# A memory-bound batch norm: phases of three tiles, stores held behind a gate, parameters loaded as rows

## The chip, the cores and the metric

The kernel runs on one core of one Trainium2 chip. The metric is the device time of one execution in microseconds; lower is better. A trace shows one execution of a kernel, so a table made from traces can differ by a few us from the medians: the traced execution of the kernel before took 2490.18 us, the slowest of its runs.

## The reference, cut to what matters

```python
# x: (32, 256, 128, 128) float32; gamma, beta, running_mean, running_var: (256,)
def reference(x, gamma, beta, running_mean, running_var):
    eps = 1e-5
    # all four reshaped to (1, -1, 1, 1)
    return gamma * (x - mean) / np.sqrt(var + eps) + beta
```

It is one multiply and one add for each element. 536.9 MB are read and as many written. A tile is 128 channels of one image: 128 rows of 16384 floats, 64 KiB a row, 8.39 MB. There are 64 tiles, and three fit on chip.

## The kernel before, the parts that matter

```python
NBUF = 3
def issue_load(i):
    t = data.tile([P, HW], mybir.dt.float32, tag="t")
    loads[i] = nc.sync.dma_start(out=t[:], in_=xr[i])
    tiles[i] = t

for i in range(NBUF):
    issue_load(i)

def load_param(ap_1d):                      # four times, 4 bytes an element
    t = params.tile([P, NCB], mybir.dt.float32, tag=ap_1d.tensor.name)
    nc.gpsimd.dma_start(out=t, in_=ap_1d.rearrange("(j p) -> p j", p=P))
    return t
# ... scale and shift from the parameters; compute(i): one tensor_scalar in place

K = NBUF - 1
for b in range((NT + K - 1) // K):
    idxs = [i for i in range(K * b, K * b + K) if i < NT]
    for i in idxs:
        compute(i)
    for i in idxs:
        store(i)                            # also on the sync queue
    for i in idxs:
        issue_load(i + NBUF)                # waits for the store of tile i
```

Loads and stores share one queue, so each of the 16 DMA engines works through them in this order: loads 0, 1, 2, stores 0, 1, loads 3, 4, stores 2, 3, and so on. I call a place where this order goes from loads to stores or back a *turn*.

## Time and profile before

| | before |
|---|---|
| time, median of 3 runs | 2487.14 us (2486.58 to 2490.18) |
| span of the profiled run | 2488.1 us |
| VectorE busy | 564.7 us, 23% |
| DMA | 9 tenths or more in all slices but the last, 432 GB/s |

From the page of the kernel before: busy times (engine, us, share, instructions), the rate in 40 equal slices, the group of the compute, and the issues with their median time from issue to landing.

```profile
DVE 564.7 (23%) x69; ACT 1.6 (0%) x2; POOL 3.2 (0%) x8
...
GB/s 414 429 438 433 433 429 437 436 430 431 435 436 433 428 437 436 434 428 436 433 437 428 435 435 435 426 437 436 435 427 435 436 438 426 434 437 436 432 431 378
...
L86 DVE TENSOR_SCALAR t<-t,scale_t,shift_t 128x16384 f32<-128x16384 f32 x64 | 564.0, 8812 | 1868.0 <-DMA t<-in_x_dram 1867.9
...
t<-in_x_dram SPq DMA_DIRECT2D x64, 38.6
out_dram<-t SPq DMA_DIRECT2D x64, 49.9
```

Nothing computes for long, VectorE waits for loads, and the rate is flat except at both ends.

The end, in windows of 4 us (window: length, three engines' busy us, clock, DMA share, GB/s):

```profile
2474.00:2478.00 4.00, 0.00 (x0) 0.00 (x0) 0.00 (x0) 1.00 0.80 344
2478.00:2482.00 4.00, 0.00 (x0) 0.00 (x0) 0.00 (x0) 1.00 0.45 197
2482.00:2486.00 4.00, 0.00 (x0) 0.00 (x0) 0.00 (x0) 1.00 0.23 98
```

The rate runs out over some 10 us, since the engines do not end together. (A packet is counted whole in the window where it begins, so single windows of a few us swing above and below 434 GB/s.)

**Splitting the packet records by engine.** The trace records each DMA packet with start, duration and bytes, but no engine number. On one engine a packet nearly always starts 3 to 4 ns before its predecessor's recorded end, and the sequence of sizes is known from the kernel's order. Chaining the records by these two rules gave 16 chains of exactly the expected length with no record left over. "Loss" is always a packet's time above the median packet of its size. In the kernel before the median 64 KiB packet takes 2.418 us, so 1024 packets an engine take 2476.0 us: that is the floor, and 12 us, 0.5%, lie above it.

### The profile page before, as it was taken

How to read it: one execution, taken by the hardware profiler on the slowest of the kernel's cores; microseconds unless marked ns; L12 is line 12 of the kernel's file. 1: busy time of each engine (PE TensorE's matmuls, PEld its weight loads, DVE VectorE, ACT ScalarE, POOL GpSimd, SP SyncE). 2: the span in 40 equal slices, each digit the busy share in tenths (PEclk: the TensorE clock that was granted, in tenths of full speed). 3: DMA queues.
4: the chain of work that ended last, by engine and by line, in shares of the span. 5: the costliest groups of instructions: out<-in, count | busy, mean ns of one | idle time of the engine just before them, and what ended most of it. 6: DMA issues, size and time to landing. Idle time of an engine off the chain costs nothing.

```text
span 2488.1 us, 378 instructions
## 1 busy us (share of the span) xinstructions
DVE 564.7 (23%) x69; ACT 1.6 (0%) x2; POOL 3.2 (0%) x8
## 2 busy tenths in 40 slices
DVE  2122211222112221122212222121221212212121
ACT  0000000000000000000000000000000000000000
POOL 0000000000000000000000000000000000000000
DMA  9999999999999999999999999999999999999998
GB/s 414 429 438 433 433 429 437 436 430 431 435 436 433 428 437 436 434 428 436 433 437 428 435 435 435 426 437 436 435 427 435 436 438 426 434 437 436 432 431 378
DMA packets 18562, 1073.77 MB, mean 432 GB/s; under 512 B 2176, under 2 KB 2176, under 8 KB 2176
## 3 DMA queue, kind: packets, MB, share of 16 engines
q1 hardware_dynamic: 18432, 1073.75, 99.8%
q0 software_dynamic: 128, 0.00, 0.0%
q14 instruction: 2, 0.02, 0.0%
HBM read 536.88 MB, written 536.87 MB: 432 GB/s over the span
## 4 chain that ended last, share of the span: by engine, by line
DMA 51%; another core or an unknown queue 36%; DVE 11%; SPq 0%; issue 0%; POOL 0%; DVEq 0%; POOLq 0%; PEldq 0%
DMA t<-in_x_dram 48%; DVE t L86 11%; DMA out_dram<-t 2%; DMA t<-in_running_mean_dram 1%; SPq L97 0%; POOL t L56 0%; DVEq L86 0%; POOLq L133 0%; SPq L48 0%; DVE shift_t L81 0%; DVE tmp_t L80 0%; DVEq L80 0%; PEldq L133 0%
## 5 line engine op out<-in xcount | busy, mean ns | idle before, releaser
L86 DVE TENSOR_SCALAR t<-t,scale_t,shift_t 128x16384 f32<-128x16384 f32 x64 | 564.0, 8812 | 1868.0 <-DMA t<-in_x_dram 1867.9
L78 DVE RECIPROCAL tmp_t<-tmp_t 128x2 f32<-128x2 f32 x1 | 0.2, 166 | 13.2 <-ACT tmp_t L71 13.2
L80 DVE TENSOR_TENSOR tmp_t<-t,scale_t 128x2 f32<-128x2 f32 x1 | 0.2, 160 | 7.6 <-DMA t<-in_running_mean_dram 7.6
L71 ACT ACT_TABLE_LOAD x1 | 1.3, 1283 | 12.4 <-DMA t<-in_running_var_dram 12.4
L79 DVE TENSOR_TENSOR scale_t<-t,tmp_t 128x2 f32<-128x2 f32 x1 | 0.2, 160 | 3.2 <-DMA t<-in_gamma_dram 3.2
L56 POOL DMA_DIRECT2D t<-in_running_var_dram x1 | 0.8, 839 | 0.8 <-PEq L133 0.8
L56 POOL DMA_DIRECT2D t<-in_gamma_dram x1 | 0.7, 722 | 0.0
L56 POOL DMA_DIRECT2D t<-in_beta_dram x1 | 0.7, 722 | 0.0
L56 POOL DMA_DIRECT2D t<-in_running_mean_dram x1 | 0.7, 722 | 0.0
L71 ACT ACTIVATE tmp_t<-t,eps_t 128x2 f32<-128x2 f32 x1 | 0.3, 295 | 0.0
L65 DVE MEMSET eps_t<- 128x1 f32 x1 | 0.1, 59 | 0.8 <-PEq L122 0.8
L81 DVE TENSOR_TENSOR shift_t<-t,tmp_t 128x2 f32<-128x2 f32 x1 | 0.2, 160 | 0.0
L122 POOL MEMSET const-bfloat16-1.0<- 128x1 bf16 x1 | 0.1, 96 | 0.0
L122 POOL MEMSET const-uint8-127<- 128x1 uint8 x1 | 0.1, 94 | 0.0
L122 POOL MEMSET const-float32-0.0<- 128x1 f32 x1 | 0.1, 93 | 0.2 <-issue 0.2
L122 POOL MEMSET const-float32-1.0<- 128x1 f32 x1 | 0.1, 93 | 0.0
## 6 DMA issues: line engine op xcount, KB each, us to landing
t<-in_x_dram SPq DMA_DIRECT2D x64, 38.6
out_dram<-t SPq DMA_DIRECT2D x64, 49.9
t<-in_running_var_dram POOLq DMA_DIRECT2D x1, 1.0 KB, 11.1
t<-in_gamma_dram POOLq DMA_DIRECT2D x1, 1.0 KB, 15.2
t<-in_beta_dram POOLq DMA_DIRECT2D x1, 1.0 KB, 19.5
t<-in_running_mean_dram POOLq DMA_DIRECT2D x1, 1.0 KB, 21.6
```

What stands on the lines that cost most here:

```text
L56: nc.gpsimd.dma_start(out=t, in_=ap_1d.rearrange("(j p) -> p j", p=P))
L65: nc.vector.memset(eps_t, eps)
L71: nc.scalar.activation(out=tmp_t[:], in_=var_t[:], func=mybir.ActivationFunctionType.Sqrt, bias=eps_t[:], scale=1.0,)
L78: nc.vector.reciprocal(out=tmp_t[:], in_=tmp_t[:])
L79: nc.vector.tensor_mul(out=scale_t[:], in0=gamma_t[:], in1=tmp_t[:])
L80: nc.vector.tensor_mul(out=tmp_t[:], in0=mean_t[:], in1=scale_t[:])
L81: nc.vector.tensor_sub(out=shift_t[:], in0=beta_t[:], in1=tmp_t[:])
L86: nc.vector.tensor_scalar(out=t[:], in0=t[:], scalar1=scale_t[:, cb : cb + 1], scalar2=shift_t[:, cb : cb + 1], op0=mybir.AluOpType.mult, ...
L122: nc = _bacc.Bacc("TRN2", target_bir_lowering=False, num_devices=1)
```

## The change

Its intent: fewer turns, three loads and then three stores; no store before all engines have nearly finished the phase's loads, so that reads and writes do not mix; and parameters read as four rows of 1 KiB instead of single floats. The core of the diff:

```diff
+GROUPS = [3] * 20 + [2, 2]
+LAST = 3072
...
+    def load_group(first, size):
+        for i in range(first, first + size - 1):
+            load(i, [HW])
+        return load(first + size - 1, [HW - LAST, HW])[0]     # two DMAs, 52 and 12 KiB a row
...
-        nc.gpsimd.dma_start(out=t, in_=ap_1d.rearrange("(j p) -> p j", p=P))
+    for r, ap in enumerate((running_var, gamma, beta, running_mean)):
+        nc.scalar.dma_start(out=rows[r : r + 1, :], in_=ap.rearrange("(o c) -> o c", o=1))
+    # ... nc.vector.transpose and four tensor_copy bring them to 128 partitions
...
+    for g, size in enumerate(GROUPS):
+        idxs = range(first, first + size)
+        for i in idxs:
+            compute(i)                                        # as many pieces as the load
+        for i in idxs:
+            s = store(i)
+            if i == first:
+                tc.add_manual_dep(s.ins, gate.ins.name, after, reason="stores after loads")
+        first += size
+        if g + 1 < len(GROUPS):
+            gate = load_group(first, GROUPS[g + 1])
```

The gate is the landing, on all 16 engines, of the 52 KiB piece of the phase's last load. When it opens, an engine that is exactly on time has eight packets of 12 KiB left, 3.7 us.

More of the change, by code (lines that the diff above doesn't have):

```diff
@@ L7 @@
 from concourse._compat import with_exitstack
-SINGLE_QUEUE = True
 NBUF = 3
+GROUPS = [3] * 20 + [2, 2]
+LAST = 3072
 @with_exitstack
@@ L26 @@
     eps = 1e-5
+    f32 = mybir.dt.float32
     N, C, H, W = x.shape
@@ L33 @@
     NT = N * NCB
+    B = 32
+    NQ = P // B
+    assert sum(GROUPS) == NT and max(GROUPS) <= NBUF
     params = ctx.enter_context(tc.tile_pool(name="params", bufs=1))
@@ L39 @@
     outr = out.rearrange("n (cb p) h w -> (n cb) p (h w)", p=P)
+    ctx.enter_context(tc.manual_schedule())
     tiles = {}
-    loads = {}
-    def issue_load(i):
-        if i >= NT:
-            return
-        t = data.tile([P, HW], mybir.dt.float32, tag="t")
-        loads[i] = nc.sync.dma_start(out=t[:], in_=xr[i])
-        tiles[i] = t
-    for i in range(NBUF):
-        issue_load(i)
-    def load_param(ap_1d):
-        t = params.tile([P, NCB], mybir.dt.float32, tag=ap_1d.tensor.name)
-        nc.gpsimd.dma_start(out=t, in_=ap_1d.rearrange("(j p) -> p j", p=P))
-        return t
@@ L59, with load @@
-    var_t = load_param(running_var)
-    gamma_t = load_param(gamma)
-    beta_t = load_param(beta)
-    mean_t = load_param(running_mean)
-    eps_t = params.tile([P, 1], mybir.dt.float32, tag="eps")
-    nc.vector.memset(eps_t, eps)
-    scale_t = params.tile([P, NCB], mybir.dt.float32, tag="scale")
-    shift_t = params.tile([P, NCB], mybir.dt.float32, tag="shift")
-    tmp_t = params.tile([P, NCB], mybir.dt.float32, tag="tmp")
+    def load(i, cuts):
+        t = data.tile([P, HW], f32, tag="t")
+        tiles[i] = t, cuts
+        return [
+            nc.sync.dma_start(out=t[:, a:b], in_=xr[i][:, a:b])
+            for a, b in zip([0, *cuts], cuts)
+        ]
@@ new lines, in load_group @@
+    def load_group(first, size):
+        for i in range(first, first + size - 1):
+            load(i, [HW])
+        return load(first + size - 1, [HW - LAST, HW])[0]
+    rows = params.tile([B, C], f32, tag="rows")
+    nc.vector.memset(rows, 0.0)
+    for r, ap in enumerate((running_var, gamma, beta, running_mean)):
+        nc.scalar.dma_start(out=rows[r : r + 1, :], in_=ap.rearrange("(o c) -> o c", o=1))
+    gate = load_group(0, GROUPS[0])
+    eps_t = params.tile([P, 1], f32, tag="eps")
@@ new lines @@
+    nc.vector.memset(eps_t, eps)
+    turned = params.tile([B, C], f32, tag="turned")
+    nc.vector.transpose(out=turned[:], in_=rows[:])
+    par = params.tile([P, NCB, 4], f32, tag="par")
+    blocks = turned.rearrange("p (cb q r) -> p cb q r", cb=NCB, q=NQ)
+    for q in range(NQ):
+        nc.vector.tensor_copy(out=par[q * B : (q + 1) * B], in_=blocks[:, :, q, 0:4])
+    var_t, gamma_t, beta_t, mean_t = (par[:, :, r] for r in range(4))
+    scale_t = params.tile([P, NCB], f32, tag="scale")
@@ L71 @@
+    shift_t = params.tile([P, NCB], f32, tag="shift")
+    tmp_t = params.tile([P, NCB], f32, tag="tmp")
     nc.scalar.activation(
         out=tmp_t[:],
-        in_=var_t[:],
+        in_=var_t,
         func=mybir.ActivationFunctionType.Sqrt,
@@ L78 @@
     nc.vector.reciprocal(out=tmp_t[:], in_=tmp_t[:])
-    nc.vector.tensor_mul(out=scale_t[:], in0=gamma_t[:], in1=tmp_t[:])
-    nc.vector.tensor_mul(out=tmp_t[:], in0=mean_t[:], in1=scale_t[:])
-    nc.vector.tensor_sub(out=shift_t[:], in0=beta_t[:], in1=tmp_t[:])
+    nc.vector.tensor_mul(out=scale_t[:], in0=gamma_t, in1=tmp_t[:])
+    nc.vector.tensor_mul(out=tmp_t[:], in0=mean_t, in1=scale_t[:])
+    nc.vector.tensor_sub(out=shift_t[:], in0=beta_t, in1=tmp_t[:])
     def compute(i):
-        t = tiles[i]
+        t, cuts = tiles[i]
         cb = i % NCB
-        nc.vector.tensor_scalar(
-            out=t[:],
-            in0=t[:],
-            scalar1=scale_t[:, cb : cb + 1],
-            scalar2=shift_t[:, cb : cb + 1],
-            op0=mybir.AluOpType.mult,
-            op1=mybir.AluOpType.add,
-        )
-    def store(i):
-        t = tiles.pop(i)
-        (nc.sync if SINGLE_QUEUE else nc.scalar).dma_start(out=outr[i], in_=t[:])
-    K = NBUF - 1
-    for b in range((NT + K - 1) // K):
-        idxs = [i for i in range(K * b, K * b + K) if i < NT]
+        for a, b in zip([0, *cuts], cuts):
+            nc.vector.tensor_scalar(
+                out=t[:, a:b],
+                in0=t[:, a:b],
+                scalar1=scale_t[:, cb : cb + 1],
+                scalar2=shift_t[:, cb : cb + 1],
+                op0=mybir.AluOpType.mult,
+                op1=mybir.AluOpType.add,
+            )
+    def store(i):
+        t, _ = tiles.pop(i)
+        return nc.sync.dma_start(out=outr[i], in_=t[:])
+    after = mybir.DependencyInfo(mybir.DependencyClass.Sync, mybir.DependencyReason.DATA)
+    first = 0
+    for g, size in enumerate(GROUPS):
+        idxs = range(first, first + size)
         for i in idxs:
@@ L104 @@
         for i in idxs:
-            store(i)
-        for i in idxs:
-            issue_load(i + NBUF)
+            s = store(i)
[4 more added lines that the diff above has]
+            gate = load_group(first, GROUPS[g + 1])
 _INS = ['x', 'gamma', 'beta', 'running_mean', 'running_var']
```

## The prediction

> **What bounds the kernel now.** The 16 DMA engines. The page's busy table gives VectorE 23% (64 x 8.81 us), the other compute engines 0%; its slices give DMA 9 tenths throughout, 432 GB/s. I split the trace's DMA packet records by engine (each packet follows the one that ended just before it). Each engine moves 1024 packets of 64 KiB. The median takes 2.418 us, loads and stores alike, so 1024 take 2476.0 us: 27.1 GB/s an engine, 434 in all. The Trainium skill (DMA: Bandwidth & Descriptors, "Where 436 GB/s comes from") puts the fabric's ceiling at 435.2 GB/s; this trace agrees within 0.4%. The span is 2488.1 us, so only some 12 us (0.5%) can be won:
> - 1.8 us before the first packet, 1.2 us after the last: they stay.
> - Packets above 2.418 us: 9.9 us on the slowest engine, 1 to 2 us on the fastest. The fastest end at 2477.7, the slowest at 2486.9 us; the windows view shows 213 GB/s and less after 2476 us.
>
> About 0.5 to 1 us an engine is lost on its first packet and another 0 to 1 us in the first 20 us, beside the parameters' 4-byte packets (the page counts 2176 under 512 B). Nearly all the rest sits in the last packet of the second load of a pair, just before stores: fast engines already store while slow ones still read, and the slow ones' packet takes 0.2 to 1.0 us more (about 0.27 us a turn over 31 turns). Turns from stores to loads cost next to nothing.
>
> **What the change does.**
> 1. Turns from loads to stores: 32 become 22. The order, one transfer after another, was already two loads, two stores.
> 2. The gate opens when the slowest engine has finished the first part of the last tile; 8 x 12 KiB an engine are left, 3.6 us at 27.1 GB/s. Landing comes 0.6 us after an engine's last packet, and issue to first packet took 1.0 us at the start, so stores reach the engines after about 1.6 us: no bubble on the slowest engine, idling only on engines that lead by over 2 us. The spread, which grew from 1.4 to 9.8 us, is held near 2 us. Mixing remains, since engines with a smaller lead still store while others read.
> 3. Splitting adds 176 packets an engine; at 9 ns or less each (what 2.418 us exceeds 65536 B at the skill's rate by; an estimate) 1.6 us.
> 4. Parameters: ready at 25 us now, perhaps 8 us after. Off the path, since loads fill the queue until 63 us; the small packets' disturbance goes, 0.5 us.
>
> **Sum.** Of the slowest engine's 8.4 us at turns, fewer turns save 2.5 us; the gate perhaps 1 to 3 more; parameters 0.5; splitting costs 1.6. I predict 2484 us (range 2479.5 to 2490). Faster by over 2%: 0.01; within 2%: 0.97; slower by over 2%: 0.02.
>
> **What would show it.** Median 64 KiB packet still 2.42 us; DMA at 9 tenths in every slice; engines' ends within 3 us, the last windows full; excess on the slowest engine 5 to 7 us, still before stores.
>
> **What would make it wrong.** If the gate's stores arrive later than 3.6 us, all engines idle 22 times. If the small spread makes reads collide with stores at every turn (0.8 us x 22), the time is 2495. If it prevents the collision, 2480.

## More of the kernel before

All runs quoted here were at a granted clock of 1.0.

A store lands 49.9 us after its issue although one transfer takes 19.3 us: it stood in the queue behind others, and the DMA engines always had work waiting.

The waits of SyncE, the engine whose queue issues all loads (L48) and stores (L97): line that waited, what for, us in total, times, longest.

```profile
SPq L48 <- DMA out_dram<-t: 1484.0, 61, 30.2
SPq L97 <- DVE t L86: 919.2, 33, 46.4
```

## The result

| | before | after |
|---|---|---|
| median of 5 runs | 2487.04 us (2486.45 to 2490.18) | 2494.43 us (2493.09 to 2495.65) |
| span of the profiled run | 2488.1 | 2493.9 |

The ratio is 1.0026, 95% interval 1.0014 to 1.0038: slower by about a quarter of a percent, well within 2%, but outside the predicted range. (A ratio is the mean time of one kernel's fast runs over that of the other's in the same rounds, so it is not quite the ratio of the medians.)

The page of the kernel after, the lines that answer to those above:

```profile
DVE 570.2 (23%) x97; ACT 1.6 (0%) x2; POOL 0.2 (0%) x4
...
GB/s 421 437 433 426 436 436 434 427 435 432 438 425 435 424 436 435 431 428 437 427 431 436 422 437 430 427 429 431 426 440 428 434 431 430 434 428 433 429 429 405
...
L103 DVE TENSOR_SCALAR t<-t,scale_t,shift_t 128x16384 f32<-128x16384 f32 (+2 forms) x86 | 568.2, 6628 | 1866.7 <-DMA t<-in_x_dram 1813.1
...
t<-in_x_dram SPq DMA_DIRECT2D x22, 6656.0 KB, 54.9
t<-in_x_dram SPq DMA_DIRECT2D x22, 1536.0 KB, 58.4
out_dram<-t SPq DMA_DIRECT2D x64, 41.9
```

The slices still look full. The last one rose from 378 to 405 GB/s, so the end is better; the middle is a little lower. Stores now land 41.9 instead of 49.9 us after issue, because they are issued later. The waits of SyncE:

```profile
SPq L114 <- DMA t<-in_x_dram: 1186.6, 22, 55.1
SPq L54 <- DMA out_dram<-t: 1026.0, 60, 19.0
SPq L114 <- DVE t L103: 182.1, 22, 8.7
```

The first line is the gate: 22 times the stores (L114) waited for a load to land. In one phase the timeline shows it (start us, us from the first issue to the end of the last, engine, line, out<-in):

```profile
1908.83 8.81 DVE L103 TENSOR_SCALAR t<-t,scale_t,shift_t 128x16384 f32<-128x16384 f32 x1 [10.56 <-DMA t<-in_x_dram]
1924.76 9.41 SPq L114 DMA_DIRECT2D out_dram<-t  x3
```

The phase's first two tiles are computed by 1917.6, but their stores are issued at 1924.8. The end:

```profile
2482.00:2486.00 4.00, 0.00 (x0) 0.00 (x0) 0.00 (x0) 1.00 0.98 426
2486.00:2490.00 4.00, 0.00 (x0) 0.00 (x0) 0.00 (x0) 1.00 0.83 360
2490.00:2494.00 4.00, 0.00 (x0) 0.00 (x0) 0.00 (x0) 1.00 0.04 16
```

The gate did what it was meant to do for the engines' unity: they now end within 2.2 us (2490.4 to 2492.6) instead of 9.2 (2477.7 to 2486.9). But the mean engine ends 9.7 us later. Where those went, in us an engine (mean of the 16), from the packet records:

```
                                              before    after
packets at the median time of their size      2476.0   2477.4
loss in the last load before stores             3.78     4.32   (both pieces of a split load)
loss in the last store before loads             0.01     6.91
loss in the first load after stores             0.09     2.10
loss elsewhere, the start included              1.22     1.21
idle (gaps over 60 ns)                          1.27     0.59
end: mean engine                              2481.3   2491.0
end: slowest engine                           2486.9   2492.6
```

Splitting costs 1.4 us. The turns from stores to loads, which had been free, cost 9.0. Evening out the engines' ends gives back 4.0 (the slowest engine was 5.6 us behind the mean and is now 1.6). What little idleness shows is no larger than before. So the question is why the last 64 KiB store packet before a load, 58 us after the gate, became slower.

Three theories:

- **Spread**: engines held close together meet each turn at the same moment and hinder each other.
- **Address**: at these turns the tile just written and the tile read next are now neighbours (k and k+1); in the kernel before they were always two apart.
- **Read-ahead**: an engine reads ahead of what it writes. When the stores are issued late, its read side has nothing to do for a moment and its lead is gone. The next reads from memory are then not hidden. The Trainium skill (DMA: Bandwidth & Descriptors, "Two DMAs through the same engine are not ordered") says that descriptors of one queue start in order but are pipelined, and that the read and the write side of an engine are separate queues; this makes such a lead possible. It states no length for it.

Read-ahead was formed after the first four runs. Their expectations still speak of a "turn theory" in its place: that an unheld turn is what costs.

### The profile page after: what moved, and what is told of

Read it like the earlier page. It is cut to its first block, busy times and chain, and to the rows that moved or that the text cites. A ratio compares the mean times of both kernels' runs of the same rounds, so it can differ in the third digit from the quotient of the medians.

```text
span 2493.9 us, 428 instructions
## 1 busy us (share of the span) xinstructions
DVE 570.2 (23%) x97; ACT 1.6 (0%) x2; POOL 0.2 (0%) x4
## 4 chain that ended last, share of the span: by engine, by line
another core or an unknown queue 72%; DVE 22%; issue 2%; DMA 2%; DVEq 0%; SPq 0%
DVE t L103 22%; DMA t<-in_x_dram 2%; DVEq L103 0%; DVEq L157 0%; SPq L54 0%
## 5 line engine op out<-in xcount | busy, mean ns | idle before, releaser
L103 DVE TENSOR_SCALAR t<-t,scale_t,shift_t 128x16384 f32<-128x16384 f32 (+2 forms) x86 | 568.2, 6628 | 1866.7 <-DMA t<-in_x_dram 1813.1
L75 DVE STREAM_TRANSPOSE turned<-rows 32x256 f32<-32x256 f32 x1 | 0.4, 432 | 21.5 <-DMA rows<-in_running_mean_dram 21.5
## 6 DMA issues: line engine op xcount, KB each, us to landing
out_dram<-t SPq DMA_DIRECT2D x64, 41.9
```

The lines of the kernel that those rows point to most:

```text
L75: nc.vector.transpose(out=turned[:], in_=rows[:])
L103: nc.vector.tensor_scalar(out=t[:, a:b], in0=t[:, a:b], scalar1=scale_t[:, cb : cb + 1], scalar2=shift_t[:, cb : cb + 1], op0=mybir.AluOpT ...
```

## Experiments

"Before" in this table is the same kernel run on the same chip in the same rounds: medians 2490.53 us for the first four runs, 2487.21 for the next four, 2487.57 for the last four, each of nine runs between 2486.1 and 2493.3.

| label | edit | median us | ratio to before, 95% |
|---|---|---|---|
| a_nogate | after, no gate | 2486.77 | 0.9989 (0.9977 to 1.0002) |
| b_params | before, parameters as rows | 2488.14 | 0.9996 (0.9983 to 1.0008) |
| a_order021 | after, tiles of a phase 0, 2, 1 | 2494.43 | 1.0021 (1.0008 to 1.0033) |
| a_hold2 | after, both turns held | 2500.26 | 1.0043 (1.0029 to 1.0057) |
| a_last2048 | after, gate at 8 KiB | 2494.06 | 1.0026 (1.0013 to 1.0038) |
| a_last4096 | after, gate at 16 KiB | 2490.51 | 1.0012 (0.9999 to 1.0025) |
| a_last6144 | after, gate at 24 KiB | 2485.94 | 0.9993 (0.9981 to 1.0006) |
| a_nosplit | after, no gate, no split | 2486.96 | 0.9997 (0.9983 to 1.0011) |
| b_gate | before, gate and split | 2505.82 | 1.0068 (1.0054 to 1.0082) |
| s2s | a_nosplit, third store held | 2508.28 | 1.0081 (1.0068 to 1.0094) |
| l2l | a_nosplit, second load held | 2524.83 | 1.0145 (1.0131 to 1.0159) |
| stagger | a_nosplit, small loads first | 2493.56 | 1.0022 (1.0009 to 1.0034) |

All gave correct results. The losses by place, us an engine, and the mean distance between the first and the last engine's end of a transfer ("spread"), from each run's packet records:

```
             last load   of it at    last store   first load    spread   slowest
             before      the first   before       after         (mean)   engine
             stores      turn        loads        stores                 ends
before         3.78        0.03        0.01         0.09        6.23    2486.9
after          4.32        0.41        6.91         2.10        1.87    2492.6
a_nogate       3.25        1.14        0.02         0.16        2.32    2483.6
b_params       4.21        1.09        0.02         0.11        5.00    2485.6
a_order021     4.25        0.77        6.49         1.39        1.97    2491.4
a_hold2        3.59        0.33        1.42        12.16        1.95    2498.8
a_last2048     0.61        0.01        8.07         1.76        0.60    2489.1
a_last4096     2.10        0.99        5.00         1.10        2.47    2487.9
a_last6144     2.73        1.12        0.02         0.16        2.86    2484.3
a_nosplit      4.42        1.13        0.00         0.05        2.91    2483.6
b_gate         5.80        0.06       11.00         3.53        2.02    2502.8
s2s           17.03        1.14        7.90         1.55        1.78    2505.4
l2l           22.54        0.87        0.00         0.27        2.60    2522.6
```

### a_nogate: the gate taken out

```diff
-            if i == first:
-                tc.add_manual_dep(s.ins, gate.ins.name, after, reason="stores after loads")
```

> The changed kernel without the gate: the stores of a phase wait for their own data alone; splitting, phases of three and parameters stay. Turn theory (the gate makes the turn from loads to stores free, and the 9 us an engine that the changed kernel loses at turns from stores to loads come from elsewhere): the last pieces of the loads lose again 0.1 us an engine a turn, the loss at the turns from stores to loads stays near 9 us an engine in the mean, and the time is the same or longer, 2493 to 2498 us. Spread theory (the gate keeps the engines within 2 us, so that all of them meet every turn at once): the spread grows to 8 us or more, the loss at the turns from stores to loads falls to under 3 us an engine, and the time falls to about 2488 us.

The loss in the last store packets went from 6.91 to 0.02 us, and the time to 2486.77. SyncE's stores now wait for VectorE, and the same phase's timeline:

```profile
SPq L114 <- DVE t L103: 1342.6, 64, 46.2
SPq L54 <- DMA out_dram<-t: 1025.3, 60, 19.1
```

```profile
1884.33 8.81 DVE L103 TENSOR_SCALAR t<-t,scale_t,shift_t 128x16384 f32<-128x16384 f32 x1 [71.92 <-DMA t<-in_x_dram]
1893.17 35.63 SPq L114 DMA_DIRECT2D out_dram<-t  x3
```

The first store is issued at 1893.2, not 1924.8: it then stands in the queue behind the phase's remaining loads. So the gate is the cause of the loss, against the turn theory, which had it stay near 9 us. But the spread, 2.32 us in the mean, hardly grew, where the spread theory had 8 us or more. In the first third of this run 14 of the engines are within 0.8 us of each other (median) at the turns from stores to loads, nearly as close as in the kernel after (0.7), and the loss there is zero. Closeness alone does not do it.

### b_params: the parameters alone

The edit is the parameter part of the diff above, put into the kernel before.

> The kernel before with the parameters as rows alone. All theories: the first three loads lose 0.3 to 0.6 us less an engine, and the time is 2486.5 us, that is 0 to 1 us under the kernel before, inside the noise. If the parameters took part in the 7 us that the change lost, the time would be above 2489 us.

2488.14 us, ratio 0.9996: no effect outside the noise. The start did get better, but the gain went at the first turn: the first two loads lost 0.70 us an engine instead of 1.14, and 1.0 us of idle gaps during the first loads went, while the third load lost 1.09 us instead of 0.03. (The 2176 small packets that the prediction puts beside the parameters are not theirs: the page counts 128 packets on their queue, q0.) In the kernel after, the parameters were not ready at 8 us as predicted: the transpose waited 21.5 us for its rows, which share the engines with the first loads (in stagger, below, where those loads were issued only at 6.9 us, it waited 3.1). That is off the critical path, since the first store can only follow three loads.

### a_order021: other neighbours at the turn

```diff
+TILE = [f + k for f in range(0, 60, 3) for k in (0, 2, 1)] + [60, 61, 62, 63]
-            nc.sync.dma_start(out=t[:, a:b], in_=xr[i][:, a:b])
+            nc.sync.dma_start(out=t[:, a:b], in_=xr[TILE[i]][:, a:b])
```

(and the same index in the scale and in the store)

> The changed kernel with the tiles of a phase taken in the order 0, 2, 1: at a turn from stores to loads the last tile written and the first tile read are then two tiles apart instead of one, as at every turn of the kernel before. Address theory (writing tile k of the output collides with reading tile k+1 of the input): the loss in the last packet of a phase's last store falls from 6.8 us an engine to under 1 us, and the time to about 2486 us. Turn and spread theories: no change, 2494 us within 1.5.

2494.43 us, loss 6.49: unchanged. The address theory falls.

### a_hold2: the other turn held too

```diff
+        s = nc.sync.dma_start(out=outr[i][:, :cut], in_=t[:, :cut])     # the phase's last store
+        if last:
+            nc.sync.dma_start(out=outr[i][:, cut:], in_=t[:, cut:])
...
+            if hold is not None and i == first:
+                tc.add_manual_dep(d.ins, hold.ins.name, after, reason="loads after stores")
```

> The changed kernel with the turns from stores to loads held in the same way: the last store of a phase in two pieces, the next phase's first load held until all engines are in the last 12 KiB a row. Turn theory (an unheld turn costs the engines that come late): the loss in the last store packets and the first load packets falls from 8.9 us an engine to under 2 us, the second split costs 1.4 us, and the time falls to about 2488 us. Spread theory: holding the engines together even more closely does not help, or hurts: 2494 to 2500 us. Address theory: the collision goes too, since a held turn keeps reads and writes apart, so this run does not tell it from the turn theory.

2500.26 us. The loss moved from the last store (now 1.42) to the first load: 12.16 us, 0.58 at each of 21 turns. Holding reads and writes further apart made it worse, which speaks against mixing as the cost of these turns; the hold has a cost of its own, though, so this run alone does not rule mixing out. This run and a_nogate gave the read-ahead theory: a load whose descriptors come late shows its delay at once; a store's shows only when loads follow.

### a_last2048, a_last4096, a_last6144: the gate moved

```diff
-LAST = 3072
+LAST = 2048        # 4096, 6144
```

> The changed kernel with the gate 8 KiB a row before the end (2.4 us of loads an engine left) instead of 12 KiB (3.6 us). Read-ahead theory (from the first four runs: an engine whose last load packet ends less than about 2 us after the stores are issued has nothing to read in between; it loses the lead of its reads over its writes, and pays 0.4 to 0.8 us in the last packet of the phase's third store, before loads): nearly every engine is now too late at every turn, the loss in those last packets rises from 6.9 to 9 to 13 us an engine, idle stretches show before the first stores, and the time is 2498 to 2505 us. Spread theory (the loss comes from engines held close together): the spread shrinks by about 1 us, the loss rises a little, 2494 to 2497 us.

> The gate 16 KiB a row before the end (4.8 us of loads left). Read-ahead theory: every engine has 1.2 us more, so that nearly all end their loads over 2 us after the issue; the loss in the last store packets falls from 6.9 to under 1.5 us an engine, and the time to about 2488 us (2486 to 2490). Spread theory: the engines are still held to a spread of about 2 to 3 us, the loss stays above 4 us an engine and the time above 2491 us.

> The gate 24 KiB a row before the end (7.3 us of loads left). Read-ahead theory: no engine runs out of reads, the loss in the last store packets is under 0.3 us an engine, the gate no longer does anything, and the time is that of the changed kernel without the gate, 2485 to 2488 us. Spread theory: the same or a little more, as the spread is still bounded; told apart by the run with 16 KiB.

The order is as read-ahead says (8.07, 6.91, 5.00, 0.02 us of loss for 8, 12, 16, 24 KiB). Two of the three expectations were wrong in size, though. At 8 KiB the loss rose only to 8.07, and the loss before stores fell from 4.32 to 0.61, so the median time hardly changed (2494.06, the ratio 1.0026 in both). At 16 KiB the loss stayed at 5.00 us and the time at 2490.51, which I had expected under the spread theory. What decided was a look at each engine by itself. For every turn and engine I took the *margin*: the end of its last load packet minus the time at which SyncE issued the phase's first store; and beside it the loss in the phase's last store packet, two transfers later. Count of engine-turns (one engine at one turn) / mean loss in ns:

```
              margin    under 1.25    1.25-1.75    1.75-2.25    over 2.25 us
a_last2048              48 / 700     182 / 378    106 / 217      0 /  -
after                   36 / 712     136 / 505     75 / 147     89 / 24
a_last4096              27 / 627     116 / 471     37 / 165    156 /  7
a_last6144               0 /  -        0 /  -       0 /  -     336 /  0
a_nogate                 0 /  -        0 /  -       0 /  -     336 /  0
```

The columns agree between kernels: what an engine loses goes with its own margin, not with where the gate stands, nor with the spread (2.47 us in a_last4096, loss 5.00; 2.32 in a_nogate, loss 0.02). An engine that still has over 2.25 us of loads in front of it when the stores are issued loses next to nothing (24 ns at most in the mean). One with less loses more the less it has. (Finer bins put the edge near 2 us: between 2.0 and 2.25 us the means are 3 to 62 ns.) Where the next loads are held too, in a_hold2, margins as short (160 engine-turns under 1.75 us) cost under 0.1 us each in the last store packet; there the loss stands in the held load. This also shows why I had the sizes wrong: the gate waits for the slowest engine, and the others lead it by more when the gate stands earlier, so the median margin was 1.66 us at 8 KiB, 1.71 at 12 and 2.08 at 16, instead of growing with the 1.2 us a step.

### a_nosplit: phases of three alone

```diff
-        return load(first + size - 1, [HW - LAST, HW])[0]
+        return load(first + size - 1, [HW])[0]
```

(and no gate)

> Phases of three and parameters as rows, without gate and without the split of each phase's last load. If the split costs what its packets cost (base sums 2478.5 against 2476.0 us in the run without the gate) the time is 1 to 2.5 us under that run, 2484 to 2486 us. If whole 64 KiB packets at the turn lose more to the other engines' stores (up to 0.9 us a packet before), the time is the same or up to 3 us longer.

2486.96 us, ratio 0.9997. Against a_nogate the base sum fell by 2.5 us to 2476.0, the loss before stores rose from 3.25 to 4.42, and the time stayed: the second possibility. (The 3.3 us that stagger's expectation names for this loss leave out the first turn.) Fewer turns with nothing else gave no gain that these runs can show.

### b_gate: the gate alone, with its split, put into the kernel before

```diff
+        cuts = [0, HW - LAST, HW] if i % 2 == 0 and i else [0, HW]
+        parts[i] = [
+            nc.sync.dma_start(out=t[:, a:b], in_=xr[i][:, a:b])
+            for a, b in zip(cuts, cuts[1:])
+        ]
...
+            s = store(i)
+            if i == idxs[0] and i + 2 in parts:
+                tc.add_manual_dep(s.ins, parts[i + 2][0].ins.name, after, reason="stores after loads")
```

(with the schedule written by hand, as in the kernel after, and the compute in the same pieces)

> The gate alone, put into the kernel before: its pairs, its one tile of lead and its parameters stay; the second load of each pair is split 52 and 12 KiB a row, and the first store of the pair waits for the first piece. Read-ahead theory: the loss comes with the gate, whatever the phase's length; engines whose loads end under 2 us after the issue pay 0.3 to 0.8 us in the last store packet before loads, 31 times, 6 to 12 us an engine (0.0 before), and the time is 2493 to 2500 us. Rival (it takes phases of three, where the next load is the neighbour of the tile just stored): the loss stays under 2 us and the time within 2 us of the kernel before.

The loss in the last store packets came, 11.00 us where it had been 0.01, with pairs and old parameters. Engine by engine it follows the same margins:

```
              margin    under 1.25    1.25-1.75    1.75-2.25    over 2.25 us
b_gate                  97 / 731     196 / 463     98 / 90     105 /  4
```

The time, 2505.82 us, is longer than expected (2493 to 2500), since the first loads lost 3.53 and the last loads 5.80 us as well, and the split cost 2.0. The gate, with the split that it needs, is enough to cause the loss; phases of three are not needed. (The split and the schedule written by hand are in a_nogate too, which has no such loss.)

### s2s and l2l: the same hold at other places

s2s holds the third store until the second is in its last 12 KiB a row; l2l holds the second load on the first in the same way. No turn is held in either. The core of s2s; l2l does the same with `load`:

```diff
+            s = store(i, size == 3 and i == first + 1)        # True: two DMAs, 52 and 12 KiB
+            if size == 3 and i == first + 1:
+                part = s
+            if size == 3 and i == first + 2:
+                tc.add_manual_dep(s.ins, part.ins.name, after, reason="third store held")
```

> Phases of three without gate and without split loads, but with the third store of a phase held until the second store has only its last 12 KiB a row left. No load waits and no turn is held. Read-ahead theory: engines again have nothing to read for a moment, this time between two stores, where reads come from on-chip memory and the delay does not show; the loss appears as before in the last packet of the third store, 4 to 9 us an engine (0.0 without the hold), and the time is 2491 to 2497 us. Turn theory (the loss comes from holding the engines together at the turn from loads to stores): nothing at the turns from stores to loads, under 1 us, and 2486 to 2489 us.

> The same hold between the first and the second load of a phase. Read-ahead theory: reads from the far memory that start late show at once, so the loss is in the first packets of the second load, 0.2 to 0.6 us a phase, 4 to 12 us an engine in all, and almost nothing (under 1 us) in the last packet of the third store; the time is 2490 to 2498 us. If any hold of all engines makes the last store packets lose, their loss is 4 us or more here too.

SyncE's waits of s2s, then of l2l, show the holds (20 and 19 times):

```profile
SPq L115 <- DMA out_dram<-t: 915.9, 20, 46.5
```

```profile
SPq L55 <- DMA t<-in_x_dram: 922.5, 19, 53.7
```

The place of the loss is as read-ahead says. With the hold between two stores, the last store packet before loads lost 7.90 us although nothing was held at a turn; only 0.34 us of idleness showed at the held store. With the hold between two loads that packet lost 0.00, so it is not any hold that does it; the delay showed at the held load itself, as 9.5 us of idle gaps and 9.9 us in its first packet, about 1.0 us a hold. Both times were far longer than expected, 2508.28 and 2524.83 us, because of something that no theory had foreseen: the last load before stores lost 17.0 and 22.5 us an engine. Without the first turn that is 0.76 and 1.03 us a turn, against 0.16 in a_nosplit. I have no explanation that a run has tested.

### stagger: a try for a faster kernel

```diff
+    for k in range(1, 16):
+        p0 = k * (k - 1) // 2
+        nc.sync.dma_start(out=dummy[p0 : p0 + k, :], in_=xr[0][p0 : p0 + k, :1536])
```

> A try for a faster kernel: phases of three, no gate, no split, and before the first load 15 small loads of 1 to 15 rows of 6 KiB into a scratch tile, which by the row count reach 1 to 15 engines, so that the engines start up to 3.4 us apart in equal steps. In the runs without gate the loss before stores fades as the engines drift into fixed offsets. If the offsets are what ends it, the loss there falls from 3.3 to under 1.5 us an engine, and the time is 2484 to 2486 us (the slowest engine carries 3.4 us more work). If not, the time is 2488 to 2491 us.

Inconclusive and slow: issuing 15 small loads delayed the first 64 KiB packet from 1.7 to 8.1 us, and the engines then started within 0.9 us of each other, so no offsets had been set. (The small loads did reach few engines: they have 120 completion packets of 4 bytes in all, 1 + 2 + ... + 15, where a full load has 16.) Its 2493.56 us less those 6.4 are about the time of a_nosplit.

No run beats the kernel before clearly. a_nogate and a_last6144 have the lowest ratios, 0.9989 and 0.9993, with intervals that include 1.

## Why the prediction was wrong, point by point

- **What bounds the kernel**: right. The median 64 KiB packet is 2.418 us in both, DMA stayed at 9 tenths, and the time stayed within 2%.
- **The spread held near 2 us, the ends within 3 us**: right, 2.2 us. It gave back 4.0 us.
- **Splitting, 1.6 us**: right, 1.4 us.
- **Fewer turns save 2.5 us**: not seen. a_nosplit loses 4.42 us an engine before stores, the kernel before 3.78. At the first turn it lost 1.13 instead of 0.03, and at the others 0.16 us a turn instead of 0.12; so there were fewer turns, but each cost more. Its time is that of the kernel before.
- **Parameters 0.5 us**: not to be told from nothing (b_params).
- **"no bubble on the slowest engine, idling only on engines that lead by over 2 us"**: this is the step that failed, and with it the term "the gate perhaps 1 to 3 more", whose sign was wrong. The arrival was estimated well: from the end of the slowest engine's first piece to the issue 0.44 us (median), and from the issue to the first packet on an engine that had run dry 0.99 us (median; 0.93 in a_last2048), 1.4 in all where I had 1.6. (The landing itself, put at 0.6 us in the prediction, comes 0.35 us after the slowest engine's last load packet in the median of the kernel before, 0.63 at most.) And hardly any idle time shows before those stores, 0.07 us an engine. But absence of idleness was the wrong test. An engine needs the next transfer issued some 2 to 2.25 us before its running load ends, by the margins, not 1.0. In the kernel after 247 of 336 engine-turns had less. They paid 0.1 to 0.7 us each, not there, but at the next turn to loads. Taking the gate out removed that loss; adding it to the kernel before produced it.
- **"excess on the slowest engine 5 to 7 us, still before stores"**: wrong. Each engine has 13.6 to 15.3 us, about half of it (6.91 in the mean) in the last store before loads.
- **"fast engines already store while slow ones still read"** as the reason for the loss before stores: open. At the first turn of a_nogate the packet records speak against it: the 16 engines lost 0.8 to 1.2 us each in the third to sixth of their 12 KiB packets, between 57.9 and 61.4 us, and no engine's first store packet began before 61.6 us. In the kernel before, the trace fits it: where eight or more engines had begun to store before a load's last packet ended, that packet lost 0.22 us in the mean (247 packets), elsewhere 0.01 (265). But nearly all of these are packets of the same eight engines, which come late at nearly every turn, and no run separates the two.
- **"If the small spread makes reads collide with stores at every turn ... 2495"**: the number was close, the reason was not. It named the turns to stores and the spread; the loss is at the turns to loads and goes with the margin.

What is shown: the gate causes the loss; each engine's loss goes with its own margin in four kernels; a hold among stores causes it and a hold among loads does not. What is argued: that a lost lead of the read side is the mechanism. It fits all of these, but no record shows the read side by itself; a queue that runs short of descriptors, for a reason other than a lead of reads, could depend on the same margin, and no run separates the two. What stays open: the loss in the last load before stores, which is 2 to 6 us in most kernels, 0.6 in a_last2048 and 17 to 23 in s2s and l2l.

## What to carry to other kernels

When the DMA engines are the bound, be wary of a hold that releases the next transfer "just in time" by the idle gaps: it can still cost, and the bill may come two transfers later. In this kernel a gate at 24 KiB a row, which left every engine over 2.25 us of loads (5.0 in the median), left 0.02 us of the loss; one at 16 KiB left 5.00 us. With at least a whole transfer standing in the queue, the kernel before lost 0.01 us there. Look at the loss per packet and per engine around the places where direction changes, since slices and idle times do not show it. Making engines end together is worth at most the distance from the mean to the slowest (5.6 us here, of which 4.0 were won), which is soon spent.

## What the Trainium skill lacked or had wrong

- DMA: Bandwidth & Descriptors, "Two DMAs through the same engine are not ordered", says that read and write side are separate and pipelined, but not how early the next transfer must be issued for an engine to lose nothing. Here: some 2 to 2.25 us before the running load's last packet ends; at 1.25 to 1.75 us, 0.4 to 0.5 us an engine are lost at the next turn from stores to loads.
- The same page, "Latency and other measured facts", gives about 0.6 us to the first byte for transfers issued from SyncE. From the start of the issue instruction to the first recorded packet on a dry engine the kernel after and a_last2048 show 0.86 us at least and 0.93 to 0.99 in the median; the two may not begin at the same point.
- The same page, "Where 436 GB/s comes from": 435.2 GB/s as ceiling; the packets here give 433.7, loads and stores alike. Agrees within 0.4%.
- No page tells that the direction of transfers matters to an engine's rate. Here a turn from stores to loads costs nothing with a full queue and up to 0.7 us an engine without one, and the last load before stores loses from 0.03 us a turn (a_last2048) to 1.0 (l2l).
